# A fused decoder step: the transpose of the maxima moved behind its step's scores, three roots moved to GpSimd, first values and sample rows issued later

## The chip, the cores and the metric

The kernel runs on one core of one Trainium2 chip. The metric is the device time of one execution in microseconds (us). The engines are PE (TensorE, matrix products), ACT (ScalarE), DVE (VectorE), POOL (GpSimd) and SP (SyncE, which issues the DMAs). Each engine works through its own queue in order, so an instruction that waits holds everything behind it on its engine.

## The reference

One layer of a hybrid decoder for two groups of rows: a prompt of 1024 tokens (8 tiles of 128) and 8 sample sequences of 4 tokens (32 rows, the ninth tile). All is float32.

1. h = RMSNorm(x) @ w_in is split into gMLP inputs u and v, a query latent cq (256), a key-value latent ckv (256) and a rope key (32). Group A is a chunked gMLP. Group B is latent attention with 8 heads of 64 + 32 dimensions: q = RMSNorm(cq) @ w_uq, k = ckv @ w_uk joined with the rope key, v = ckv @ w_uv, with an RMSNorm of q and k per head, a rotation of the last 32 dimensions, and a softmax. Prompt rows attend causally to the prompt. The rows of each sample attend to 4096 cached positions (32 pages of 128 from a page table) and to themselves. Both groups' outputs are RMS-normalised, joined and multiplied with w_o.
2. Memory attention, 4 heads, 256 memory tokens.
3. A gated FFN with a causal convolution of width 3.

Outputs are both groups' rows, and the new latents, keys and states.

## The kernel before

Float32 products are made of three matmuls each (`mm3`, L179-185): both operands are split into a rounded high part and the low rest (`split`, L187-202: the high part on ACT, the low part on DVE), and high x high, high x low, low x high are summed in PSUM. Nearly all rows of PE in the profile therefore have line L185. Reciprocal roots are made from simple operations by `rsqrt_steps` (L214-245): with no engine given, 11 operations on DVE; with GpSimd given, 3 on DVE and 13 on GpSimd.

The stages, in order: phase 1 (norms, w_in, gMLP), phase 2a (prompt attention), phase 2b (sample attention over the cache), output projection, memory attention, FFN. The change touches phases 2a and 2b. In the other stages a scheduler sets the order when the kernel is built; in the two loops below the order on PE, ACT, DVE and POOL is the order of the code.

**Start of phase 2a (L596-655).** `proj_group` (L795-858) returns two lists for a group of tiles and four heads (hf 0 or 1): first queries and keys with their squares, norms and rotations, and second the values (6 matmuls of 128x256 for each tile, copied from PSUM by ACT, L815). For hf 0 all groups, (0,2), (2,4), (4,6), (6,8) and the sample rows (8,9), run both lists here, with PSUM tiles of the tag "mm" (5 buffers). Then the pools ps1 and p2x are closed, ps2 is opened, and `head_prep` (L860-876) transposes keys and queries of head 0 on PE (L872; two times four tiles each) and splits them. `proj_weights` for hf 1 follows, with its splits (w q and w v, low parts on DVE, L192).

**The attention loop of phase 2a.** 32 units (head, pair of query tiles) are worked through in 80 slots t. A slot of the loop issues transposes of the probabilities (L918, copied to pth by ACT, L920), the scores of the unit two ahead (L185, tile s; the maximum and the copy on DVE, L899 and L903; the exponential on ACT, L909), the products with the values (L930), and whatever stands in `extra[t]`, where `spread` puts head preparations and the projections of hf 1. POOL makes weight sums for the FFN (L770-773) in every fourth slot from 22 on. When 28, 29 and 30 units are done, a *mixer* (`mix_steps`, L1479-1505) starts for G = 0, 2 and 1: ACT squares two tiles with a sum per row (L1490), the root of the 128x2 sums (mixr) is made on DVE, ACT scales by it (L1496), PE transposes (L1501), DVE copies (L1502), and SP stores the result. These three are the only calls that give the arguments z = 1 and a function nt.

**Phase 2b (L1048-1169).** 8 batches of 16 steps, n from -10 on; step n scores two pages (`pair_score`: 12 matmuls of 128x288 into the two banks of tile s, then 12 of 128x256 into a third, tile s2; each tag has two buffers). `at(n, pos, f)` registers f for a position of a step, and a step runs: positions -2, -1, 0, the rotation of a coming quad's keys, position 1, the step's scores, position 2, in every fourth step 8 products with the cached latents (`quad_pv`, L1348), position 3. What pair_score leaves for the next step (the rope copy L1253, and the sums ss of L1278) runs at position -1 of it. The rope matmul L1250 of every second step writes into the new tile s.

The softmax of a batch is spread over steps by `batch_softmax` (L1282-1339) in eleven parts r, at the positions of L1082, counted from the batch's first step: r = 0 to 3 norms and scaling of pages 0 to 23, r = 4 their maxima, r = 5 and 6 the same for the rest (ends with the joined maxima mx, L1323), r = 7 the transpose of the maxima on PE (L1326), r = 8 on DVE their maximum over partitions (L1329) and a diagonal matrix dg (L1331), r = 9 on PE a matmul that broadcasts it (L1334), an ACT copy bc (L1336) and a subtraction on POOL (L1337), r = 10 the exponential on ACT. Parts that fall behind the last step go to a list `late` in their order; that is so from r = 7 on for the last batch.

Of the kernel before, what the change touches and what calls it, by code (L numbers as in the profile page):

```python
# [154 lines left out]
class Net:  # L155
# [440 lines left out]
    def phase2a(self):  # L596
        nc, tc, I, O = self.nc, self.tc, self.I, self.O
        p = self.open("p2q")
# [4 lines left out]
        p = self.open("p2")  # L603
        pp = self.pools["ps1"][1]
        px = self.open("p2x")
        heads = lambda: {"v": self.t(p, [P, 8, 4, 64], F32, "v", 2)}
        st = [{**heads(), **self.wqv}]
# [34 lines left out]
        rq = self.t(p, [P, 8, 8], F32, "rq")  # L642
        c = {"ggq": ggq, "cmask": cmask, "rq": rq, "kss": kss, "qt": qt}
        groups = ((0, 2), (2, 4), (4, 6), (6, 8), (8, 9))
        for g in groups:
            for f in sum(self.proj_group(p, pp, 0, *g, st[0], c, ("mm", 5)), []):
                f()
        self.close("p2x")
        self.close("ps1")
        pp = self.open("ps2", space=PSUM)  # L650
        pm = self.open("p2m")
        for f in self.head_prep(pm, pp, 0, st[0], c):
            f()
        st.append({**heads(), **self.proj_weights((pm, [P, 512], F32, "pth", 5), 1)})


# [2 lines left out]
        def spread(fs, t0, t1):  # L659
            for j, f in enumerate(fs):  # L660
                extra[t0 + j * (t1 - t0) // len(fs)].append(f)

        for h in (1, 2, 3, 5, 6, 7):
            fs = self.head_prep(pm, pp, h, st[h // 4], c)
            if h == 3:
                for f, t in zip(fs, (13, 14, 15, 19)):
                    extra[t].append(f)
            else:
                spread(fs, max(0, 10 * h - 16), 10 * h - 8 if h > 1 else 3)
        late = [self.proj_group(p, pp, 1, *g, st[1], c) for g in groups]  # L670
        for (q, _), t in zip(late, ((16, 20), (18, 23), (21, 26), (24, 29))):
            spread(q, *t)
# [7 lines left out]
        with tc.manual_schedule(engines={E.PE, E.Activation, E.DVE, E.Pool}):  # L680
# [30 lines left out]
            for n, u in enumerate(units):  # L711
                nu = units[n + 2] if n + 2 < len(units) else None
                k = u["n"]
# [334 lines left out]
    def phase2b(self):  # L1048
        nc, tc, I = self.nc, self.tc, self.I
        pa = self.pa3 = self.open("p3a", side="right")  # L1050
        pt, p = self.open("p3t"), self.open("p3")
        ppt, pp = self.open("ps3t", space=PSUM), self.open("ps3", space=PSUM)
# [11 lines left out]
        st, ev, late = {}, {}, []  # L1064

        def at(n, pos, f, *a):
            ev.setdefault((n, pos), []).append(lambda: f(*a))
# [10 lines left out]
        for b in range(NB):  # L1078
            n = b * 16
            at(n - 10, 0, lambda b: st.__setitem__(b, self.batch_open(p, b)), b)  # L1080
            at(n - 8, 2, lambda b: self.batch_enter(st[b], b), b)
            for r, (k, pos) in enumerate(((12, 0), (13, 0), (14, 0), (14, 3), (15, 0), (16, 0), (16, 2), (18, 0), (18, 3), (19, 2), (20, 2))):  # L1082
                f = lambda b=b, r=r: self.batch_softmax(p, ppt, st[b], r, b == NB - 1)
                if n + k <= last:
                    at(n + k, pos, f)
                else:
                    late.append(f)
            n += 16 + LAG + 15
            tail = (
                lambda b=b: self.batch_out(pt, st[b], 0),  # L1090
                lambda b=b: self.batch_out(pt, st[b], 1, ppt),
                lambda b=b: self.batch_close(pt, ppt, b, st.pop(b)),
            )
            for k, pos, f in ((0, 3, tail[0]), (1, 2, tail[1]), (3, 3, tail[2])):
                if b < NB - 1:
                    at(n + k, pos, f)
# [382 lines left out]
    def mix_steps(self, p, pp, z, i0, i1, src, hl, nt, tt):  # L1479

        nc = self.nc
        t0, tn, m = TILES[i0][0], TILES[i1 - 1][1], i1 - i0
        r = self.t(p, [P, 2], F32, "mixr", 2)[:tn, :m]
        ns = []
        for i in range(i0, i1):

            n = nt(i - i0)[:tn] if nt else src(i)[:tn]
            ns.append(n)
            o = n if nt else hl[:, 2 * (i - i0) : 2 * (i - i0) + 2].rearrange("p k n -> p (k n)")[:tn]
            nc.scalar.activation(o, src(i)[:tn], AF.Square, accum_out=r[:, i - i0 : i - i0 + 1])  # L1490
        yield
        self.rsqrt(p, r, r, 1.0 / 512)
        w = m * tn
        yield
        for i, n in enumerate(ns):
            nc.scalar.activation(n, src(i0 + i)[:tn], AF.Copy, scale=r[:, i : i + 1])  # L1496
        yield
        for i, n in enumerate(ns):
            tp = self.t(pp, [P, 512], F32, *tt).rearrange("p (k n) -> p k n", k=4)[:, :, :tn]
            for k in range(4):  # L1500
                nc.tensor.transpose(tp[:, k], n[:, k * P : k * P + P], self.ident[:tn, :tn])  # L1501
            nc.vector.tensor_copy(hl[:, :, i * tn : i * tn + tn], tp)  # L1502
            if nt is None and i < m - 1:
                yield
        nc.sync.dma_start(self.mix_dram[:, z * 4 : z * 4 + 4, t0 : t0 + w], hl[:, :, :w])
# [779 lines left out]
```

## Time and profile before

| | |
|---|---|
| median of 3 runs | 1880.57 us (1879.95 to 1886.6) |
| the profiled execution | 1887.48 us |
| its span, first to last instruction | 1885.8 us |
| mean granted TensorE clock | 0.985 |
| PE busy | 1822.9 us |
| DVE, ACT, POOL busy | 1380.2, 927.5, 715.1 us |
| phase 2a, first score of the loop | at 221.7 us |
| phase 2b, one batch of 16 steps | 57.40 us |

Times in the profile are us from the first instruction. A row of a timeline gives start, length, engine, line, operation, "output<-inputs" by the program's names, partitions x elements, a count, and in brackets how long the engine was idle before it and which instruction ended that. PEclk is the share of full speed that TensorE's clock was granted. PEld is PE's loading of weights, beside its matmuls. Lines are those of the kernel before.

### The profile page before, as it was taken

To read this page: it belongs to the slowest core of one execution; us is meant where nothing else is said; L and a number is where in the kernel's file an instruction comes from. 1 tells how busy PE (TensorE), PEld (TensorE's weight loads), DVE (VectorE), ACT (ScalarE), POOL (GpSimd) and SP (SyncE) were. 2 spreads that over 40 slices of the span, in tenths; PEclk is the share of its full clock that TensorE was granted. 3 is DMA by queue.
4 is the path that set the end of the run, shared out by engine and by line. 5 is a ranking of instruction groups with operands and counts; after the bars stand their busy time and mean duration, and the time that the engine had idled before them with its cause. 6 is when DMAs were issued, how large, how long until landed. Compare 5 with 4: busy or idle time off the path is not lost.

```text
span 1885.8 us, 39848 instructions
## 1 busy us (share of the span) xinstructions
PE 1822.9 (97%) x14402; PEld 1757.2 (93%) x14402; DVE 1380.2 (73%) x2883; ACT 927.5 (49%) x1965; POOL 715.1 (38%) x826
## 2 busy tenths in 40 slices
PE   6999899989999999999999999999999999999999
PEld 6999799889999999998799988999999999999999
DVE  6865967766777667776654676788888888879664
ACT  6435676666555555555443355633332333344442
POOL 1221515643544455444213100157677677500000
PEclk9999899999999999999999999999999999999999
DMA  8102204666765665664564335322222222395252
GB/s 294 60 10 69 80 1 163 228 223 186 213 196 167 187 179 169 175 170 148 171 177 134 134 134 163 128 80 69 91 69 94 77 69 80 99 363 164 79 153 76
DMA packets 135559, 260.18 MB, mean 138 GB/s; under 512 B 20417, under 2 KB 78626, under 8 KB 132290
## 3 DMA queue, kind: packets, MB, share of 16 engines
q1 hardware_dynamic: 134498, 256.58, 43.4%
q8 instruction: 114, 1.87, 0.4%
q10 hardware_dynamic: 864, 1.05, 0.2%
q14 instruction: 83, 0.68, 0.1%
HBM read 212.27 MB, written 45.30 MB: 137 GB/s over the span
## 4 chain that ended last, share of the span: by engine, by line
PE 60%; DVE 6%; issue 4%; DMA 3%; POOL 2%; SPq 1%; ACT 1%; POOLq 0%; DVEq 0%; ACTq 0%
PE d L185 12%; PE s L185 11%; PE b L185 7%; PE F L185 7%; PE X L185 6%; PE E L185 6%; PE A L185 3%; PE y L185 3%; DMA cT<-cT 1%; PE o L1348 1%; DVE mx L1299 1%; POOL S L1296 1%; PE t L185 1%; PE v L185 1%; SPq L1207 1%
## 5 line engine op out<-in xcount | busy, mean ns | idle before, releaser
L185 PE MATMUL s<-w2h,ch 128*128 128x288 f32 (+1 forms) x1024 | 303.8, 297 | 0.0
L185 PE MATMUL s<-w2h,cl 128*128 128x288 f32 (+1 forms) x1024 | 295.1, 288 | 2.7 <-POOL cl L1235 1.4
L185 PE MATMUL s<-w2l,ch 128*128 128x288 f32 (+1 forms) x1024 | 294.7, 288 | 0.0
L185 PEld LDWEIGHTS s<-w2h,ch 128*128 128x128 f32 x1024 | 192.6, 188 | 10.8 <-issue 8.3
L185 PEld LDWEIGHTS s<-w2h,cl 128*128 128x128 f32 x1024 | 192.4, 188 | 3.4 <-POOL cl L1235 1.9
L185 PEld LDWEIGHTS s<-w2l,ch 128*128 128x128 f32 x1024 | 192.8, 188 | 0.0
L1278 DVE TENSOR_REDUCE ss<-sq 128x16 f32<-128x1024 f32 x128 | 155.6, 1215 | 49.3 <-ACT sq L1275 48.4
L1235 POOL TENSOR_TENSOR cl<-cT,ch 128x512 fp32r<-128x512 f32 x64 | 83.7, 1307 | 160.7 <-ACT ch L1231 128.9
L1275 ACT ACTIVATE sq<-s 128x512 f32<-128x512 f32 x128 | 76.5, 598 | 90.0 <-PE s L185 90.0
L1272 ACT ACTIVATE sq<-s 128x512 f32<-128x512 f32 x128 | 76.8, 600 | 78.0 <-PE s L185 78.0
L191 ACT CAST a<-brb 128x528 fp32r<-128x528 f32 x77 | 48.8, 634 | 111.0 <-PE d L185 107.1
L185 PE MATMUL mm<-whi,xh 128*128 128x256 f32 (+3 forms) x288 | 84.5, 294 | 14.4 <-ACT xh L195 9.8
L185 PE MATMUL d<-a,w 128*128 128x264 f32 x768 | 95.4, 284 | 1.0 <-DVE G L2064 1.0
L192 DVE TENSOR_TENSOR a<-brb,a 128x528 fp32r<-128x528 f32 x77 | 54.4, 707 | 57.2 <-ACT a L191 57.1
L185 PEld LDWEIGHTS d<-a,w 128*128 128x128 f32 x768 | 94.3, 188 | 1.1 <-issue 1.1
L185 PE MATMUL mm<-wlo,xh 128*128 128x256 f32 (+3 forms) x288 | 83.3, 292 | 0.0
L185 PE MATMUL mm<-whi,xl 128*128 128x256 f32 (+3 forms) x288 | 83.2, 293 | 0.0
L930 PEld LDWEIGHTS o<-v,pth 128*128 128x128 f32 x576 | 75.9, 197 | 7.3 <-ACT pth L920 5.2
L930 PE MATMUL o<-v,pth 128*128 128x64 f32 x576 | 76.2, 274 | 4.8 <-ACT pth L920 4.4
L1935 POOL TENSOR_TENSOR lo<-s,hi 128x1024 fp32r<-128x1024 f32 x20 | 63.0, 3148 | 45.7 <-ACT hi L1934 45.7
L1231 ACT CAST ch<-cT 128x512 fp32r<-128x512 f32 x128 | 73.5, 627 | 3.9 <-DMA cT<-cT 3.9
L1990 ACT COPY a<-A 128x264 f32<-128x264 f32 x43 | 16.1, 375 | 118.7 <-PE A L185 114.9
(714 smaller groups left out, 6472.2 us busy)
## 6 DMA issues: line engine op xcount, KB each, us to landing
cT<-cT SPq DMA_DIRECT2D x256, 160.0 KB, 2.5
ck<-ck SPq DMA_DIRECT2D x256, 144.0 KB, 3.4
raw<-w_up SPq DMA_DIRECT2D x44, 512.0 KB, 3.6
wsumd<-wsum SPq DMA_DIRECT2D x13, 1024.0 KB, 4.3
actd<-cv SPq DMA_DIRECT2D x44, 264.0 KB, 2.6
brb<-actd SPq DMA_DIRECT2D x44, 264.0 KB, 5.9
wsum<-w_down SPq DMA_DIRECT2D x11, 1024.0 KB, 5.2
raw<-wsumd SPq DMA_DIRECT2D x20, 512.0 KB, 3.8
```

What stands on the lines that cost most here:

```text
L185: self.nc.tensor.matmul(out, l, r, start=first and i == 0, stop=last and i == len(seq) - 1)
L191: {"act": nc.scalar.copy, "pool": nc.gpsimd.tensor_copy, "dve": nc.vector.tensor_copy}[eng](hi, src)
L192: low = lambda: nc.vector.tensor_tensor(lo, src, hi, ALU.subtract)
L930: nc.tensor.matmul(u["o"][:, e], th[:, z * P : z * P + P], s["v"][:, jj, h % 4], start=j == z == 0, stop=e == 1 and jj == 2 * G + 1)
L1207: nc.sync.dma_start(ck[j * 32 : j * 32 + 32], I["ck"][bass.ds(rv, 1)].rearrange("a t s f -> (a t) s f"))
L1231: nc.scalar.copy(d["h"][:, k], src[k])
L1235: (nc.vector if k else nc.gpsimd).tensor_tensor(d["l"][:, k], src[k], d["h"][:, k], ALU.subtract)
L1272: nc.scalar.activation(sq[:, 0], ps[:, :, n0 : n0 + 256], AF.Square)
L1275: nc.scalar.activation(sq[:, 1], pt.rearrange("p (e d) -> p e d", e=2), AF.Square)
L1278: yield lambda: nc.vector.tensor_reduce(s["ss"][:, g0 : g0 + 2].rearrange("p e (z h) -> p z e h", z=2), sq.rearrange("p z e (h d) -> p z e ...
L1296: e.tensor_tensor(x, x, ss[:, g0:g1].rearrange("p g h -> p (g h)").unsqueeze(2).broadcast_to([P, n, 4]), ALU.mult)
L1935: eng.tensor_tensor(lo, src, hi, ALU.subtract)
```

## The change

Four edits. (1) For hf 0 only queries and keys of the groups (0,2) to (6,8) run before the pools change; their values run behind the preparation of head 0, in the PSUM tag "tp" (4 buffers). (2) The sample rows' queries and keys for hf 0 are spread over the slots 4 to 11 of the attention loop. (3) In the softmax of a batch, part 7 goes from step 18, position 0 to position 2; part 8 from step 18, position 3 to step 19, position 1; part 9 from step 19, position 2 to step 20, position 0; part 10 from step 20, position 2 to position 3. (4) The three late mixers of phase 2a make their roots with `rsqrt_steps` on GpSimd.

```diff
-        for g in groups:
-            for f in sum(self.proj_group(p, pp, 0, *g, st[0], c, ("mm", 5)), []):
+        for g in groups[:4]:
+            for f in self.proj_group(p, pp, 0, *g, st[0], c, ("mm", 5))[0]:
                 f()
         self.close("p2x")
         self.close("ps1")
...
         for f in self.head_prep(pm, pp, 0, st[0], c):
             f()
+        for g in groups[:4]:
+            for f in self.proj_group(p, pp, 0, *g, st[0], c)[1]:
+                f()
         st.append({**heads(), **self.proj_weights((pm, [P, 512], F32, "pth", 5), 1)})
...
+        spread(self.proj_group(p, pp, 0, 8, 9, st[0], c)[0], 4, 12)
         late = [self.proj_group(p, pp, 1, *g, st[1], c) for g in groups]
...
-            for r, (k, pos) in enumerate(((12, 0), (13, 0), (14, 0), (14, 3), (15, 0), (16, 0), (16, 2), (18, 0), (18, 3), (19, 2), (20, 2))):
+            for r, (k, pos) in enumerate(((12, 0), (13, 0), (14, 0), (14, 3), (15, 0), (16, 0), (16, 2), (18, 2), (19, 1), (20, 0), (20, 3))):
...
-        self.rsqrt(p, r, r, 1.0 / 512)
+        for _ in self.rsqrt_steps(p, r, r, 1.0 / 512, nc.gpsimd if z and nt else None):
+            pass
```

## The prediction

> **What bounds the kernel now.** I read the page's busy shares first, then the waits of PE, then the stretches in which those waits lie. The page:
>
> ```profile
> PE 1822.9 (97%) x14402; PEld 1757.2 (93%) x14402; DVE 1380.2 (73%) x2883; ACT 927.5 (49%) x1965; POOL 715.1 (38%) x826
> ```
>
> PE (the matrix engine) is busy 97% of the 1885.8 us span, so all that is left to win without removing matmuls is some 63 us of holes, and time at a reduced clock. None of the four edits removes a matmul. The waits of PE (us in total, times, longest):
>
> ```profile
> PE m L1326 <- DVE mx L1323: 6.3, 7, 0.9
> PE o L930 <- ACT pth L920: 4.4, 1, 4.4
> PE tp L872 <- DVE rqa L234: 2.3, 1, 2.3
> ```
>
> The first is the transpose of the maxima, once for each of 7 batches. The second lies where the three late mixers stand. The third lies at the start of the attention, behind the first values and the sample rows. So each edit touches a known hole, and I price each hole alone.
>
> **Edit 3, the maxima.** Steps 49 to 52 of batch 2, PE, then DVE, ACT and POOL (start, length, operation):
>
> ```profile
> 610.84 0.28 PE L185 MATMUL s<-w2h,cl 128*128 128x256 f32 x1
> 612.06 0.29 PE L1326 MATMUL m<-ident,mx 128*32 128x128 f32 x1 [0.94 <-DVE mx L1323]
> 615.18 0.38 PE L1250 MATMUL s<-bd,krq 128*128 128x128 f32 x2
> 618.49 0.40 PE L1334 MATMUL m<-dg,ones 32*128 32x32 f32 x2
> 618.83 1.07 PE L1348 MATMUL o<-ck,S 128*32 128x257 f32 x16
> 619.83 0.40 PE L185 MATMUL s<-w2h,ch 128*128 128x288 f32 x1
> ...
> 613.92 0.21 DVE L1274 TENSOR_TENSOR S<-s,S 128x64 f32<-128x64 f32 x1
> 616.45 0.33 DVE L1331 TENSOR_SCALAR dg<-ident,mm 32x32 f32<-32x32 f32 x1
> 617.01 0.71 DVE L1235 TENSOR_TENSOR cl<-cT,ch 128x512 fp32r<-128x512 f32 x1 [0.23 <-issue]
> 617.64 1.21 DVE L1278 TENSOR_REDUCE ss<-sq 128x16 f32<-128x1024 f32 x1
> 618.77 0.27 DVE L1244 TENSOR_REDUCE kss<-ksq 128x4 f32<-128x128 f32 x1
> ...
> 614.16 0.27 ACT L1253 COPY S<-s 128x128 f32<-128x128 f32 x1 [2.41 <-DVE S L1274]
> ```
>
> The transpose (position 0 of step 50) stands ahead of step 50's scores and waits 0.94 us for the maxima; 24 score matmuls are queued behind it. Moved to position 2 it stands behind them, and the maxima have 3 us to spare. But the 0.94 us does not all come back. Step 51 begins with L1250, which writes a scores buffer; there are two, and the one it takes is free when ACT's rope copy L1253 has read step 49's (614.16 + 0.27 = 614.43). That copy waits for DVE's addition at 613.92, which the edit does not make earlier. Without the hole L1250 would come at 615.18 - 0.94 = 614.24, so it now waits until about 614.5: gain so far 0.68.
>
> The diagonal dg (r = 8) goes from position 3 of step 50 to position 1 of step 51, behind cl, ss and kss: 617.01 to 619.04 in the rows above. As its own 0.6 us now follow them, dg ends at about 619.06 less the part of the 0.68 that DVE's operations follow: 618.6 to 619.06, I take 618.95. The broadcast L1334 (r = 9) goes behind the value matmuls of L1348, which end about 618.83 + 1.0 - 0.34 (the broadcast that no longer precedes them) - 0.68 = 618.8. So the broadcast starts at about 618.95, takes 0.34, and step 52 starts at about 619.25 instead of 619.83: gain 0.6. Over 7 batches (the last batch's steps are in the late list, unmoved): **-4.2 us**. The ends are -6.6 (the whole wait, 7 x 0.94) and 0 (the rope copy and dg eat it all). A loss I exclude here: the exponentials are first read some three steps later, 9 us at the 3.1 us from L1326 to L1250, while copy, subtraction and exponential come to this:
>
> ```profile
> 619.35 2.48 POOL L1337 TENSOR_TENSOR S<-S,bc 128x1056 f32<-128x1056 f32 x1 [1.27 <-ACT bc L1336]
> ```
>
> and an exponential of the same tile on ACT, at most as much again. Behind the waiting transpose stands nothing but the rest of PE's queue, and it no longer waits.
>
> **Edit 4, the roots on GpSimd.** At the end of the attention loop, ACT, DVE (the first row groups the three roots' first operations: min/median/max ns, first and last start), POOL and PE:
>
> ```profile
> 418.15 1.32 ACT L1496 ACTIVATE k<-b_all,mixr 128x512 f32<-128x512 f32 x2
> 420.60 1.04 ACT L920 COPY pth<-tp 128x512 f32<-128x512 f32 x2
> 425.90 1.33 ACT L1496 ACTIVATE k<-b_all,mixr 128x512 f32<-128x512 f32 x2
> 429.66 1.34 ACT L1496 ACTIVATE k<-b_all,mixr 128x512 f32<-128x512 f32 x2
> ...
> L222 DVE TENSOR_SCALAR rqx<-mixr x3: 158/169/170, 411.5 to 425.6; 128x2 f32<-128x2 f32 x3
> 414.48 0.16 DVE L236 SCALAR_TENSOR_TENSOR mixr<-rqh,rqy 128x2 f32<-128x2 f32 x1
> ...
> 417.20 1.27 POOL L773 TENSOR_TENSOR wsum<-wsum 128x512 f32<-128x512 f32 x1
> 418.49 0.45 POOL L1220 TENSOR_TENSOR krq<-cT,cosT 128x128 f32<-128x128 f32 x1
> ...
> 421.21 1.08 PE L930 MATMUL o<-v,pth 128*128 128x64 f32 x4 [4.43 <-ACT pth L920]
> ```
>
> The first late mixer's root is ready at 414.64 on DVE; ACT reads it at 418.15 (L1496), then squares for the next mixer, then copies pth, for which PE sits idle 4.43 us. From ACT's L1496 to PE's end of idling are 3.06 us in a fixed order. Each root keeps 3 of its 11 DVE operations and gets 13 on GpSimd: 3 x 8 = 24 DVE operations go, 39 GpSimd ones come. In the order of the changed kernel all 39 stand behind the last weight sum, which ends at 417.20 + 1.27 = 418.47. So the root that was 3.5 us early is now late by whatever its 13 operations take, and L1496 holds ACT, pth and PE behind it.
>
> No GpSimd operation on 128x2 stands in this trace. The nearest rows, a copy of 128x16 (min/median/max ns) and two steps of a root on 128x64:
>
> ```profile
> L2044 POOL COPY S<-state x22: 193/198/573, 1210.1 to 1608.0; 128x16 f32<-128x16 f32 x22
> ...
> 909.99 0.32 POOL L243 TENSOR_TENSOR rqh<-rqh,rqa 128x64 f32<-128x64 f32 x1
> 910.40 0.37 POOL L244 TENSOR_SCALAR rqh<-rqh 128x64 f32<-128x64 f32 x1
> ```
>
> 0.45 for 128 elements and 0.32 for 64 make about 0.2 at 2 elements, as the copy has it; the two steps start 0.41 apart, 0.09 beyond the first one's length, so I take 0.28 apart. The first root is then ready at 418.47 + 13 x 0.28 = 422.1, L1496 is 3.95 late, and PE with it. The second root starts when its squares are done, about 420.7 as pth follows them at 420.60, and has 425.90 - 420.7 = 5.2 us for 3 DVE operations (0.6) and 13 on GpSimd (3.6), so it is in time; the third has 429.66 - 425.6 = 4.0 and is 0.2 late. **+4.1 us.** Ends: 0.16 apart, a DVE operation's length, gives +2.4; 0.41 apart, as at 128x64, gives 418.47 + 5.3 = 423.8, +5.65, and the third root is then 1.9 late, +7.6 in all. That DVE is freed earlier brings nothing, as ACT waits for the root, not for DVE. The Trainium skill (GPSIMD Engine Reference, section 3.1) has a tensor_tensor on GpSimd 1.96 times as long as on VectorE, in a measurement with large tiles; by that and DVE's rows here, about 0.32 to 0.4 apart, this term would be an estimated +4.5 to +5.7 instead; no run here shows it at two elements.
>
> **Edits 1 and 2, the start of the attention.** Stretches, in busy us of PE, PEld, DVE, ACT, POOL, then PEclk (granted clock), DMA share and GB/s:
>
> ```profile
> 216.50:221.40 4.90, 2.34 (x10) 1.87 (x10) 4.87 (x26) 1.99 (x5) 1.13 (x1) 0.50 0.02 9
> 221.40:226.00 4.60, 4.33 (x14) 3.50 (x15) 4.57 (x21) 1.88 (x6) 0.00 (x0) 0.50 0.00 0
> 226.00:233.50 7.50, 7.50 (x30) 6.87 (x29) 5.00 (x18) 3.22 (x7) 1.46 (x4) 0.50 0.01 2
> 417.00:421.20 4.20, 0.00 (x0) 0.00 (x0) 0.70 (x4) 4.20 (x10) 2.73 (x6) 1.00 0.47 199
> 421.20:428.10 6.90, 6.88 (x34) 6.89 (x34) 4.65 (x23) 3.63 (x9) 0.00 (x0) 0.51 0.31 109
> ```
>
> DVE is full up to 226 and PE waits for it; the clock is half from 216.5 to 233.5. Before, the values (48 matmuls) lie inside this DVE-bound stretch and cost nothing; after, they stand among the first scores, where PE is full:
>
> ```profile
> 211.23 0.28 PE L185 MATMUL mm<-wvh,ckh 128*128 128x256 f32 x1
> 211.94 0.33 PE L185 MATMUL mm<-wqh,cqh 128*32 128x384 f32 x1
> 221.72 0.46 PE L185 MATMUL s<-kTh,qTh 96*128 96x128 f32 x1
> 234.42 0.37 PE L185 MATMUL s<-kTh,qTl 96*128 96x448 f32 x1
> ```
>
> The first row is the first of the last value's six matmuls, the second follows them: 0.71 us, 0.118 each, so 48 make 5.7 us at full clock. The sample rows' 12 matmuls (211.94 to 213.84) move 1.9 us of PE into the loop as well; there they displace nothing but PE's own queue. In return the first score needs neither the last keys' transposes, nor the sample rows' chain, nor the weight splits ahead of it on DVE; counting those (some 4 to 6 us of the chain that ends at 221.40), I put it at 216.0 instead of 221.72. From the first score to the row at 234.42 PE had 12.7 us of work, 11.8 of it at half clock: 5.9 + 0.9 = 6.8 at full clock. With 5.7 + 1.9 it is 14.4. If the half clock lasts 6.9 us as at 421.20, until 222.9, 3.45 of the 14.4 are done by then and the rest takes 10.95, to 233.85 instead of 234.42: **-0.6 us**. The ends: the 12.1 us that it lasted after 221.40 give 216.0 + 12.1 + 8.35 = 236.45, +2.0; a clock that never drops gives 230.4, -4.0. The Trainium skill (TensorE: Matmul & The Clock Gate, Part 1) says that the first 3.4 us or so of activity run at half clock and everything after at full; the stretches above show 6.9 and 12.1. By that rule the term would be an estimated -2.3, between this forecast and the third rival.
>
> **The rest.** The output projection and the memory attention hold the same instructions in a slightly other order that the scheduler chose; I see no sign for either, 0 with ±3.
>
> Sum: -4.2 + 4.1 - 0.6 = **-0.7 us**. The profiled execution took 1887.5 (1885.8 of span, 1.7 around it) and would take 1886.8; the median of the three runs is 1880.57, lower by 7, and since the edits' terms are short waits and not shares, I take them off it unscaled: **1879.9 us**.
>
> **Rivals.**
> - *The GpSimd roots cost more* (ends on the slower side). One mechanism: each small operation on GpSimd takes as long as at 128x64. Then edit 4 is +7.6 and the sum +2.8: 1883.4. It decides from about 0.30 us apart: 0.32 + 13 x 0.30 = 4.2 and the third root's 0.5 make 4.7, against the 4.8 that the other edits give. For it: the rows at 128x64; against: the copy's 0.2. Beside busy DVE work the same root's steps took much longer (min/median/max ns):
>
> ```profile
> L239 POOL TENSOR_TENSOR rqa<-rqa,rqx x2: 1185/1246/1307, 899.3 to 906.1; 128x64 f32<-128x64 f32 x2
> ```
>
> So long, the first root alone would make 13 x 1.25 = 16 and a sum of +12: 1892; but DVE does nearly nothing in 417.00:421.20.
> - *The maxima's wait only changes its name.* Rope copy, dg and the DVE backlog behind them end at the same time as before; edit 3 gives 0, the sum is +3.5: 1884.1. For it: dg is now behind 2 us of DVE work. Against: DVE stood idle ahead of cl.
> - *The clock stays up at the attention's start*, since PE pauses less: -4.0 instead of -0.6, sum -4.1: 1876.5; with the cheap ends of the other two, -6.6 + 2.4 - 4.0 = -8.2, 1872.4.
>
> **How the numbers follow.** Forecast 0.45, dear roots 0.25 (of which 0.05 for 1892), renamed wait 0.15, clock 0.15 (of which 0.05 near 1872). Predicted is the likeliest, 1879.9. The range from 1872 to 1888 holds all but about 0.2: the ends of the terms together, -11 and +13 (with the 3 of the rest), less their least likely corners. A measurement here tells about 0.5%, 9.4 us, from no change. Faster by more than that needs all gains at once: 0.07; slower by more needs the dear roots under traffic, or a transfer pushed back in a queue: 0.10; within: 0.83.
>
> **What the changed kernel's profile would show.** Right: the wait at L1326 gone, small ones at L1250 (for ACT's rope copy) and at the broadcast (for dg), step 52 about 0.6 earlier after step 49; PE's wait for pth about 8 us instead of 4.43, with ACT's scaling waiting for a POOL result; first score near 216, half clock to about 223. Wrong: the wait for pth under 7 us or over 10; a batch as long as before, 57.40 us for 16 steps in this row:
>
> ```profile
> 599.00:656.40 57.40, 56.46 (x479) 53.12 (x478) 42.25 (x81) 32.11 (x72) 27.59 (x43) 1.00 0.64 177
> ```
>
> It would also be wrong if the output projection moved by more than 3 us.

## The result and the profile after

The changed kernel takes 1888.3 us (median of 13 runs; two of them, at 5.2 and 6.2 ms, were disturbed and stand outside the comparison, and the other 11, 1886.07 to 1891.78, have the median 1888.1). The kernel before takes 1884.0 us (13 runs, 1879.95 to 1886.71). The ratio of the two, without those two runs, is 1.0027, 95% interval 1.0017 to 1.0037: **slower by 5.1 us** (0.0027 x 1884), 3.2 to 7.0. Forecast was -0.7 us.

The page of the changed kernel's profile (span 1885.5 us) and its waits of PE (us in total, times, longest). Its lines are numbered four or five higher than before: the transpose is L1330, cl L1239, the wait for pth L934, the rope matmul L1254.

```profile
PE 1819.1 (96%) x14402; PEld 1755.0 (93%) x14402; DVE 1377.8 (73%) x2859; ACT 927.2 (49%) x1965; POOL 722.6 (38%) x865
```

```profile
PE s L185 <- DVE cl L1239: 7.1, 7, 1.3
PE o L934 <- ACT pth L924: 7.0, 1, 7.0
...
PE tp L876 <- DVE k L852: 3.4, 1, 3.4
PE s L1254 <- DVE rsum L939: 2.6, 1, 2.6
```

The 7 waits for the maxima (6.3 us) are gone; 7 waits for cl (7.1 us) stand in their place. The wait for pth grew from 4.4 to 7.0. At the first rope matmul of the sample attention PE now waits 2.6 us, where before it waited 1.26 for a cl a little further on:

```profile
437.24 0.40 PE L185 MATMUL s<-w2h,cl 128*128 128x288 f32 x1 [1.26 <-DVE cl L1235]
```

So each of the holes has a successor as large or larger.

**Batch 2, steps 50 to 52 of the changed kernel**, DVE, then PE and ACT:

```profile
614.45 0.19 DVE L1327 TENSOR_TENSOR mx<-mx 128x32 f32<-128x32 f32 x1
614.62 0.69 DVE L1239 TENSOR_TENSOR cl<-cT,ch 128x512 fp32r<-128x512 f32 x1
616.55 0.21 DVE L1278 TENSOR_TENSOR S<-s,S 128x64 f32<-128x64 f32 x1
621.08 0.23 DVE L1335 TENSOR_SCALAR dg<-ident,mm 32x32 f32<-32x32 f32 x1
```

```profile
615.37 0.40 PE L185 MATMUL s<-w2h,cl 128*128 128x288 f32 x1 [0.98 <-DVE cl L1239]
617.81 0.27 PE L1330 MATMUL m<-ident,mx 128*32 128x128 f32 x1
617.92 0.39 PE L1254 MATMUL s<-bd,krq 128*128 128x128 f32 x2
621.24 1.07 PE L1352 MATMUL o<-ck,S 128*32 128x257 f32 x16
622.24 0.41 PE L1338 MATMUL m<-dg,ones 32*128 32x32 f32 x2
```

The low half cl of a quad is made in two parts, the first on POOL and the second on DVE (`quad_prep`). The sixth matmul of step 50, the row at 615.37, is the first to read the second part, and DVE makes that part directly behind the last operation on the maxima. Before, the transpose waited for the maxima and cl was ready a moment later; now five scores go ahead of the transpose, and the sixth waits 0.98 us for cl, where the transpose waited 0.94.

What this does to a batch is read from broadcast to broadcast, with one trap. In the kernel before the broadcast stands ahead of the value matmuls of its step, in the changed kernel behind them (621.24, then 622.24 above). The first batch has no values of an earlier batch there, so between its first two broadcasts the kernel before has three sets of 16 value matmuls and the changed one four (55.63 and 57.09 us). Between later broadcasts both have four: the mean of these five times is **57.53 us instead of 57.44**. The mean over all six, 57.46 instead of 57.14, counts the extra set as a loss.

**The late mixers of the changed kernel**, POOL, ACT, DVE and PE:

```profile
411.30 1.27 POOL L777 TENSOR_TENSOR wsum<-wsum 128x512 f32<-128x512 f32 x1
412.52 0.20 POOL L238 TENSOR_TENSOR rqa<-rqy 128x2 f32<-128x2 f32 x1
415.99 0.19 POOL L245 TENSOR_TENSOR mixr<-rqh,rqy 128x2 f32<-128x2 f32 x1
```

```profile
416.22 1.33 ACT L1501 ACTIVATE k<-b_all,mixr 128x512 f32<-128x512 f32 x2 [2.74 <-POOL mixr L245]
...
428.24 1.33 ACT L1501 ACTIVATE k<-b_all,mixr 128x512 f32<-128x512 f32 x2 [0.68 <-POOL mixr L245]
```

```profile
433.87 1.29 DVE L1507 COPY v<-tp 128x512 f32<-128x512 f32 x2 [4.32 <-DMA mix<-v]
```

```profile
419.30 1.97 PE L934 MATMUL o<-v,pth 128*128 128x64 f32 x8 [7.01 <-ACT pth L924]
435.30 0.46 PE L1254 MATMUL s<-bd,krq 128*128 128x128 f32 x2 [2.61 <-DVE rsum L939]
```

The first root begins on POOL when the last weight sum ends, takes 3.66 us (412.52 to 416.18), and ACT waits for it. The third is 0.68 late. Behind them the last mixer's copy out of PSUM waits for the DMA that stores an earlier one, and the first rope matmul waits until that copy and what follows it on DVE (rsum, at 435.07) are done.

**The attention's start in the changed kernel** (columns as before; PEclk is the third from the end):

```profile
204.00:207.00 3.00, 3.00 (x14) 3.00 (x13) 3.00 (x14) 1.15 (x3) 2.46 (x7) 0.50 0.82 226
211.00:214.00 3.00, 1.90 (x8) 1.45 (x8) 2.86 (x10) 0.38 (x1) 2.44 (x4) 0.50 0.89 359
214.00:221.00 7.00, 6.65 (x32) 6.63 (x32) 4.57 (x18) 2.49 (x7) 0.62 (x1) 0.52 0.00 1
221.00:226.00 5.00, 5.00 (x42) 4.85 (x41) 2.20 (x7) 3.57 (x13) 0.00 (x0) 1.00 0.00 0
```

```profile
214.36 0.47 PE L185 MATMUL s<-kTh,qTh 96*128 96x128 f32 x1 [0.35 <-ACT qTh L195]
230.95 0.37 PE L185 MATMUL s<-kTh,qTl 96*128 96x448 f32 x1
```

The first score comes 7.4 us earlier (214.36 for 221.72), the scores of 448 columns 3.5 us earlier (230.95 for 234.42).

### The profile page after: what moved, and what is told of

It is laid out like the page before. It is cut to its first block, busy times and chain, and to the rows that moved or that the text cites. A ratio compares the mean times of both kernels' runs of the same rounds, so it can differ in the third digit from the quotient of the medians.

```text
span 1885.5 us, 39860 instructions
## 1 busy us (share of the span) xinstructions
PE 1819.1 (96%) x14402; PEld 1755.0 (93%) x14402; DVE 1377.8 (73%) x2859; ACT 927.2 (49%) x1965; POOL 722.6 (38%) x865
## 4 chain that ended last, share of the span: by engine, by line
PE 63%; DVE 5%; issue 4%; DMA 2%; POOL 2%; SPq 1%; ACT 1%; DVEq 0%; POOLq 0%; ACTq 0%
PE s L185 12%; PE d L185 12%; PE b L185 8%; PE X L185 7%; PE F L185 7%; PE E L185 7%; PE A L185 3%; PE y L185 3%; PE o L1352 1%; DVE mx L1303 1%; POOL S L1300 1%; DMA cT<-cT 1%; PE t L185 1%; PE v L185 1%; PE s L1254 0%
## 5 line engine op out<-in xcount | busy, mean ns | idle before, releaser
L1239 POOL TENSOR_TENSOR cl<-cT,ch 128x512 fp32r<-128x512 f32 x64 | 83.2, 1300 | 150.8 <-ACT ch L1235 135.8
L934 PEld LDWEIGHTS o<-v,pth 128*128 128x128 f32 x576 | 75.0, 196 | 9.6 <-ACT pth L924 7.8
L934 PE MATMUL o<-v,pth 128*128 128x64 f32 x576 | 75.6, 273 | 7.1 <-ACT pth L924 7.0
```

What stands on the lines that cost most here:

```text
L934: nc.tensor.matmul(u["o"][:, e], th[:, z * P : z * P + P], s["v"][:, jj, h % 4], start=j == z == 0, stop=e == 1 and jj == 2 * G + 1)
L1239: (nc.vector if k else nc.gpsimd).tensor_tensor(d["l"][:, k], src[k], d["h"][:, k], ALU.subtract)
```

## The experiments

**Which edit costs.** Each edit was put alone into the kernel before.

e1, edit 3 alone:

```diff
-(18, 0), (18, 3), (19, 2), (20, 2)
+(18, 2), (19, 1), (20, 0), (20, 3)
```

> The kernel before with edit 3 alone (the maxima's transpose and what follows it later). Theory A: the low half cl of the next quad stands right behind the maxima on DVE, so step 50's third matmul waits for it as long as the transpose waited before: no wait at L1326, 7 waits of about 1 us for cl (7.1 us in the changed kernel), each batch 0.0 to 0.2 us longer; in all 0 to +1 us. Theory B, as predicted: the maxima's wait was the limit, edit 3 gives -4.2 us, and what the changed kernel lost it lost to the roots and at the start of the sample attention: -3 to -5 us.

Measured: ratio 1.0005 (0.9992 to 1.0018), +0.9 us (-1.5 to +3.4); waits for cl 7.9 us (8, one of them at the start of the sample attention), none at the transpose; a batch 57.50 us (mean of five, as above), 0.06 longer. Theory A, but that it is the sixth matmul that waits; the forecast's -4.2 is excluded.

e2, edit 4 alone:

```diff
-        self.rsqrt(p, r, r, 1.0 / 512)
+        for _ in self.rsqrt_steps(p, r, r, 1.0 / 512, nc.gpsimd if z and nt else None):
+            pass
```

> The kernel before with edit 4 alone (three roots on GpSimd). Theory A: 13 operations 0.28 us apart behind the last weight sum; PE's wait for pth 7.0 to 8.4 us instead of 4.4, the third root some 0.7 late: +2.5 to +4.5 us. Theory B: the late roots only fill time that PE would lose anyway at the start of the sample attention (where the first quads' loads and the last mixer's store end): 0 to +1 us.

Measured: 1.0017 (1.0006 to 1.0028), +3.2 us. Theory A, with a longer wait than expected; the wait for cl at the start of the sample attention also grew, from 1.26 to 2.23 us, as the last mixer's copy comes later. POOL, ACT and PE:

```profile
413.83 1.26 POOL L773 TENSOR_TENSOR wsum<-wsum 128x512 f32<-128x512 f32 x1
415.05 0.19 POOL L238 TENSOR_TENSOR rqa<-rqy 128x2 f32<-128x2 f32 x1
...
418.74 1.33 ACT L1497 ACTIVATE k<-b_all,mixr 128x512 f32<-128x512 f32 x2 [6.72 <-POOL mixr L245]
...
421.81 1.97 PE L930 MATMUL o<-v,pth 128*128 128x64 f32 x8 [9.36 <-ACT pth L920]
```

e3, edits 1 and 2; e8, edit 1 alone; e9, edit 2 alone:

```diff
-        for g in groups:
-            for f in sum(self.proj_group(p, pp, 0, *g, st[0], c, ("mm", 5)), []):
+        for g in groups[:4]:                                  # e3, and e8 with the sample rows behind it
+            for f in self.proj_group(p, pp, 0, *g, st[0], c, ("mm", 5))[0]:
...
+        for g in groups[:4]:                                  # in place of `for g in groups`, both lists: e9
...
+        for g in groups[:4]:                                  # behind head_prep: e3, e8
+            for f in self.proj_group(p, pp, 0, *g, st[0], c)[1]:
...
+        spread(self.proj_group(p, pp, 0, 8, 9, st[0], c)[0], 4, 12)   # e3, e9
```

> The kernel before with edits 1 and 2 (values and sample rows later). Theory A: 3.4 us won at the scores of 448 columns, of which the sample rows' 12 matmuls take back 1.8; the ten more PSUM tiles of the tag tp turn its four buffers by two, so that the first rope matmul of the sample attention now waits about 2.6 us for the last mixer's copy out of its bank (in the changed kernel that wait is 2.6): +0.5 to +1.5 us in all. Theory B: that wait comes from the late roots and is absent here: -1.5 to -2 us.

> The kernel before with edit 1 alone (first values behind the first transposes; sample rows where they were). Theory A (values move from a stretch where PE waits for DVE into one where PE is full; the first scores come earlier by as much): between -1 and +1 us. Theory B (the values' place is what loses: PE has nothing to do while DVE works, so its clock halves earlier): +1 to +3 us, with half clock from about 203 on.

> The kernel before with edit 2 alone (sample rows into the loop's slots 4 to 11). Theory A: DVE's chain to the first score loses the sample rows' operations, some 2 us, and PE gets 1.8 us more in the loop: -1 to +0.5 us. Theory B (PE's 1.8 us is all that counts): +1.5 to +2 us.

Measured: both 1.0010 (0.9998 to 1.0021), values alone 1.0021 (1.0010 to 1.0031), sample rows alone 1.0034 (1.0021 to 1.0046). Each half alone costs more (+4.0 and +6.4 us) than both together (+1.9); the expectations for the halves failed but for theory B of the values: half clock comes at 204.5, and its +1 to +3 us overlaps the interval (1.9 to 5.8). The wait at the first rope matmul is there in e3 with the roots on DVE, as theory A has it, but 1.47 us long. Where it stands fits the number of new tiles of the tag tp, which has four buffers: e8 adds eight, two whole turns, and has no such wait (1.25 for cl, as before); e9 adds two and e3 ten, half a turn more, and have it, as do all seven profiles with edit 2 and none of the twelve without. The rows of e3 and e9:

```profile
435.83 0.46 PE L1254 MATMUL s<-bd,krq 128*128 128x128 f32 x2 [1.47 <-DVE rsum L939]
```

```profile
433.90 0.46 PE L1251 MATMUL s<-bd,krq 128*128 128x128 f32 x2 [0.88 <-DVE v L1503]
```

That turn costs some 0.2 us against the 1.25, so it is not what the halves cost; why they do not add is not settled.

**The maxima.** e5 puts part 6 (up to the joined maxima) behind cl as well; e11 moves the transpose alone, e12 part 6 alone; e10 adds to e5 one addition on POOL instead of DVE:

```diff
 positions of r = 6, 7, 8, 9, 10
-(16, 2), (18, 0), (18, 3), (19, 2), (20, 2)      # before
+(17, -1), (18, 2), (19, 1), (20, 0), (20, 3)     # e5, e10
+(16, 2), (18, 2), (18, 3), (19, 2), (20, 2)      # e11
+(17, -1), (18, 0), (18, 3), (19, 2), (20, 2)     # e12
...
-            e.tensor_tensor(x, x, s["kss"][:, g0:g1]...
+            (nc.gpsimd if g0 else e).tensor_tensor(x, x, s["kss"][:, g0:g1]...     # e10
```

> The kernel before with edit 3, and in addition part 6 of the softmax (the rest of the norms up to the joined maxima) one step later, step 17 position -1, so that cl stands ahead of the maxima on DVE; the transpose at step 18 position 2 still comes behind them. Theory A: the waits for cl go with those for the maxima; each batch is 0.6 to 0.95 us shorter, -4 to -6.5 us in all. Rival: the rope copy behind DVE's backlog and dg hold PE instead, 0 to -2 us, with waits named S (ACT) or dg (DVE).

> The kernel before with only the transpose of the maxima moved (part 7 to step 18, position 2; parts 8 to 10 where they were). Read from the time between two batches' broadcasts (57.13 us before, 57.35 with all of edit 3 alone). Theory A (PE waits for cl as long as it waited for the maxima, and the excess comes from dg and the broadcast behind step 51): 57.1 to 57.2. Theory B (the transpose itself in the new place costs): 57.3 to 57.4.

> The kernel before with only part 6 of the softmax moved behind cl, the transpose at its old place ahead of step 50's scores. Theory A (two results of one DVE queue are needed at the start of step 50, and whichever is last holds PE): the transpose now waits longer, 1.2 to 1.8 us instead of 0.94, and a batch takes 57.3 to 58.0 us. Theory B (cl alone was the limit): 56.7 as with both moved.

> The kernel of the run before with the maxima behind cl, and in addition the first addition of the second norms (1.1 us on DVE in its profile) on POOL, which is idle there. Theory A (what is left of the wait, 2.3 us at L1250 for ACT's rope copy, comes from DVE's backlog): that wait falls to under 0.5 us and the time is 1.5 to 2.5 us under that run's, -5 to -6 us against the kernel before. Theory B (the backlog follows PE and refills): the same -3 us as without it.

Measured, by the last five times between broadcasts: before 57.44 us a batch, e11 57.50, e1 57.50, e12 57.92, **e5 56.82**, e10 57.15. (The expectations count from the mean of all six; for e11 and e12 that changes nothing, as their broadcast stands in the old place.) So the transpose alone gains nothing, nor does all of edit 3; part 6 alone loses 0.5; both together gain 0.62 a batch, 4.3 us over 7. e5's ratio is 0.9983 (0.9970 to 0.9996), -3.2 us (-5.7 to -0.8): theory A by the batch, with the waits that the rival named in the place of those for cl. One wait was held by two results of one queue. DVE, ACT and PE of e5:

```profile
607.40 0.68 DVE L1235 TENSOR_TENSOR cl<-cT,ch 128x512 fp32r<-128x512 f32 x1
610.20 0.19 DVE L1323 TENSOR_TENSOR mx<-mx 128x32 f32<-128x32 f32 x1
611.63 0.21 DVE L1274 TENSOR_TENSOR S<-s,S 128x64 f32<-128x64 f32 x1
...
611.88 0.27 ACT L1253 COPY S<-s 128x128 f32<-128x128 f32 x1 [2.15 <-DVE S L1274]
...
611.93 0.27 PE L1326 MATMUL m<-ident,mx 128*32 128x128 f32 x1
612.29 0.46 PE L1250 MATMUL s<-bd,krq 128*128 128x128 f32 x2
```

cl is 3 us ahead now, and what is left is what the forecast had named: the rope copy and dg. Waits of PE in e5, 490 to 900 us, then, from the whole span, e12's at the transpose and e11's for cl:

```profile
PE s L1250 <- ACT S L1253: 2.3, 6, 0.9
PE m L1334 <- DVE dg L1331: 0.7, 1, 0.7
```

```profile
PE m L1326 <- DVE mx L1323: 10.5, 7, 2.0
```

```profile
PE s L185 <- DVE cl L1235: 8.0, 8, 1.5
```

e10 failed: the wait for the rope copy rose to 3.9 us (7) where it should have gone, and the ratio is 1.0004 (0.9994 to 1.0015). DVE waits for the addition on POOL (7 times, 2.9 us between 490 and 900), and the first step of the root behind it then runs beside POOL's half of cl and takes 1.26 or 1.27 us in each of the seven batches, where it took 0.35 in six of them in e5 (0.20 in the first, with POOL idle). DVE of e10, then of e5:

```profile
607.79 1.26 DVE L222 TENSOR_SCALAR rqx<-ss 128x64 f32<-128x64 f32 x1 [0.41 <-POOL ss L1289]
```

```profile
605.16 0.35 DVE L222 TENSOR_SCALAR rqx<-ss 128x64 f32<-128x64 f32 x1
```

**The roots' place in the queue.** e7 has edit 4 and every weight sum four slots earlier; e14 the earlier sums alone:

```diff
-            wsums = dict(zip(range(22, 75, 4), (NK, NK + 1, *range(NK))))
+            wsums = dict(zip(range(18, 71, 4), (NK, NK + 1, *range(NK))))
```

> The kernel before with edit 4, and every weight sum four slots earlier, so that the last one is over before the first root comes to POOL. Theory A (the roots are late because they stand behind the last weight sum; 13 operations at 0.28 us cost 1.5 us more than DVE's 11, which the slack holds): PE's wait for pth falls from 9.4 us with edit 4 alone to some 4 to 6, and the time comes within 1 us of the kernel before. Theory B (the operations themselves are too slow on POOL, wherever they stand): PE's wait stays over 8 us and the time stays 3 us above.

> The kernel before with the weight sums four slots earlier and nothing else. Theory A (the gain of the run with all edits and both repairs lies in the sums' place: a weight sum on POOL no longer falls where the loop's end needs POOL, DVE or the port they share): -2 to -4 us. Theory B (earlier sums alone change nothing; they only let the roots on GpSimd pay): -1 to +1 us.

Measured: e7 1.0008 (0.9994 to 1.0021), e14 1.0006 (0.9995 to 1.0017). The interval of e7 overlaps that of e2 (1.0006 to 1.0028), so the repair shows in the waits and not in the time. In e7 the sum is over 2 us before the first root, and PE's wait for pth is 2.6 us and 1.0 us instead of 9.4. POOL and PE of e7:

```profile
406.27 1.29 POOL L773 TENSOR_TENSOR wsum<-wsum 128x512 f32<-128x512 f32 x1
409.78 0.19 POOL L238 TENSOR_TENSOR rqa<-rqy 128x2 f32<-128x2 f32 x1 [2.22 <-DVE rsum L935]
...
416.55 1.10 PE L930 MATMUL o<-v,pth 128*128 128x64 f32 x8 [2.63 <-ACT pth L920]
```

The operations are the same, so what made the wait was the queue, not the engine. Sums alone gain nothing that shows (theory B).

**Mended versions.** e6: edits 1, 2 and 3 with part 6 behind cl. e13: all four edits, part 6 behind cl, earlier sums. e15: e13 without edit 4. e16: e13 without edits 1 and 2. Their lines are those above, in these combinations:

```diff
+ r = 6 at (17, -1)                 # e6, e13, e15, e16
+ wsums from range(18, 71, 4)       # e13, e15, e16
- roots on GpSimd                   # left out: e6, e15
- values and sample rows later      # left out: e16
```

> The changed kernel without the roots on GpSimd (edits 1, 2 and 3) and with part 6 of the softmax behind cl. If the parts add, by the medians of the runs alone: +1.9 (edits 1 and 2) - 3.2 (maxima behind cl) = -1.3 us, -4 to +1. If edits 1 and 2 cost nothing by themselves and their +1.9 was chance: -3.2.

> All four edits with both repairs: part 6 of the softmax behind cl, and the weight sums four slots earlier, so that the roots on GpSimd do not stand behind the last one. If the parts add: +1.9 - 3.2 + 1.5 (roots with earlier sums) = +0.2 us, -3 to +3, against +5.1 for the four edits as they are. PE's wait for pth under 5 us; batch 56.7 us.

> Edits 1, 2 and 3 with maxima behind cl and sums four slots earlier, roots on DVE: the best run without edit 4. Theory A (roots on GpSimd gain nothing by themselves): -5 to -7 us, as with them. Theory B (once they do not stand behind a weight sum the roots on GpSimd gain, as DVE's scores and value scalings no longer stand behind a root): -1 to -3 us, 4 us above the run with them.

> Edits 3 and 4 with both repairs, and the start of the attention as before (without edits 1 and 2). If edits 1 and 2 cost the +1.9 us of their run alone, this one is 2 us under the run with all four, -8 to -10 us. If they cost nothing or gain beside the others: -5 to -7 us.

Measured: e6 0.9995 (0.9980 to 1.0011), e13 **0.9962 (0.9949 to 0.9976), -7.1 us**, e15 1.0020 (1.0010 to 1.0030), e16 0.9999 (0.9986 to 1.0012). e6 is as the sum of the parts has it. e13 beats the kernel before and the sum (+0.2) by 7 us and the changed kernel, by the two ratios, by 12 (e13 ran on one chip, e15 and e16 on another, each beside the kernel before); taking out either the roots on GpSimd or the new start loses all of that. For e15 theory B holds in direction; for e16 neither does. All four kernels have a batch of 56.8 us (56.76 to 56.87, mean of five), so the batches do not tell them apart. What does is not found: the profile of e13 is of an execution that took 1884.4 us, 5.6 above the median of its runs, and can't show where its gain lies.

**The same kernels profiled once more.**

```diff
 (no change: e17 is the kernel before, e18 the changed one)
```

> The kernel before, profiled once more, to see what of a stage's time belongs to the code and what to the clock. Theory A (the half clock comes in whole steps of some 3.4 us whose start is free, so stages with a hole in PE vary from run to run by 1.7 us a step, and the others do not): against the first profile the attention's start, the stretch around 310, the mixers and the output projection differ by up to 3 us each, batches (57.14) and the FFN by under 0.1. Theory B (the stages' times belong to the code): all within 0.3 us.

> The changed kernel, profiled once more. Theory A: its mixers' stage is again some 4 us longer than that of kernels with roots on DVE and its batches again 57.4 to 57.5 us, while the attention's start and the output projection move by up to 3 us against its first profile. Theory B: all stages within 0.3 us of its first profile.

The table gives how much longer a stage of PE took than in the first profile of the kernel before, measured between the same two matmuls (named by their times there).

| kernel | 160 to 281: start | 281 to 360 | 409 to 480: mixers | 480 to 880: batches | 880 to 1000: out |
|---|---|---|---|---|---|
| before again (e17) | -2.5 | -1.3 | -1.6 | +0.1 | -0.5 |
| changed | -0.8 | -2.9 | +6.1 | +1.0 | -3.2 |
| changed again (e18) | -0.8 | -1.3 | +4.3 | +1.7 | -1.7 |
| e1, edit 3 | -2.6 | -1.3 | +3.0 | +1.2 | -2.5 |
| e2, edit 4 | -2.5 | -1.3 | +4.6 | +0.4 | -2.1 |
| e3, edits 1 and 2 | -2.1 | +0.2 | +1.3 | +0.3 | +0.7 |
| e5 | -2.4 | -1.3 | +0.7 | -2.3 | -2.0 |
| e6 | -2.0 | +0.2 | +4.7 | -3.5 | -1.3 |
| e9, edit 2 | +0.4 | +0.2 | -1.8 | +1.0 | +1.6 |
| e13 | +1.4 | +0.9 | -2.6 | -3.3 | +1.8 |
| e15 | +1.2 | +0.8 | -1.1 | -2.2 | -0.6 |
| e16 | -0.4 | +2.3 | -1.8 | -4.0 | +1.3 |

Theory A holds for both in these stages. One kernel's stages with a hole in PE differ by up to 2.5 us between two executions; its batches agree (57.44 and 57.41, mean of five; changed 57.53 and 57.55). The stretches of e17 that answer to the first row of the changed start above and to those shown in the prediction:

```profile
204.00:207.00 3.00, 2.09 (x13) 2.04 (x14) 2.90 (x9) 3.00 (x20) 3.00 (x8) 1.00 0.82 224
221.40:226.00 4.60, 4.60 (x16) 3.79 (x16) 4.06 (x21) 2.08 (x6) 0.00 (x0) 0.50 0.00 0
226.00:233.50 7.50, 7.50 (x47) 6.77 (x46) 5.98 (x19) 5.91 (x13) 1.46 (x4) 0.92 0.01 2
```

In the first profile the last of these was at 0.50 throughout. Differences of up to some 2.5 us in a stage with a hole are therefore no evidence from one profile. The mixers' stage shows edit 4 only on the mean: 5.0 in the three profiles with the roots behind the weight sum (6.1, 4.3, 4.6), 1.2 in the eleven with the roots on DVE and the sums in their old places (-1.8 in e9 to +4.7 in e6), so 3.8, near the forecast 4.1.

## Why the prediction was wrong

The sign and the size of the sum failed, at one step above all, and the time lies just above the range. From the median of 13 runs the same sum gives 1883.3, and the range moves up with it: the baseline decided on which side of the bound the time fell, but not the sign.

- **Edit 3 (-4.2 forecast, the step that failed).** The prediction has "24 score matmuls are queued behind it" and "the maxima have 3 us to spare", and never asks what those matmuls themselves need. The sixth of them needs the part of cl that DVE makes right behind the maxima, and waits 0.98 us for it. So PE is not released 0.94 us earlier, from which the step reckoned on. Measured: +0.1 us a batch in the changed kernel, +0.06 in e1, and +0.9 us (-1.5 to +3.4) for edit 3 alone, so the term was about 5 us too low. A batch as long as before was the sign of being wrong that the prediction itself had named. The rival that the wait would only change its name came true (0.15 was given), by cl and not by the rope copy or dg. What the step said of those two was right: with cl out of the way e5 waits for just them and gains 0.62 a batch, against the forecast 0.6.
- **Edit 4 (+4.1).** Right in mechanism and size: 13 operations in 3.66 us (forecast 3.64), behind the last weight sum, PE's wait 7.0 (forecast about 8), third root 0.68 late (0.2). Alone it measured +3.2 (1.1 to 5.3), and with the sum out of the way the wait shrank to 2.6. GpSimd at two elements costs 0.19 to 0.23 us and 0.28 apart, as the row of 128x16 gave; the dearer rival had the wrong neighbour, and the 1.96 that the Trainium skill (GPSIMD Engine Reference, section 3.1) gives for large tiles does not carry down to two elements: a tensor_tensor took 0.19 to 0.20 us on GpSimd and 0.16 on DVE, 1.2 times.
- **Edits 1 and 2 (-0.6).** The first score came even earlier than forecast (214.36 for 216.0) and the half clock ended at about 221 (222.9). But the gain was reckoned against an execution whose half clock lasted 17 us; in e17 it ended some 6 us sooner (0.92 in the last row above is 1.2 us of half clock), and the start of the kernel before took 2.5 us less. Against that one the changed start loses 1.7 us (-0.8 against -2.5). The term also put the half clock at 6.9 us from the first score on. In the changed kernel it lasted 10.2 us, from 210.5 to 220.7, and 3.4 us more from 203.7, ahead of the first score, where the prediction has none: with the values gone PE was busy 2.06 us from 200 to 204, against 3.45 in e17. All seven profiles with edit 1 have half clock between 200 and 208, none of the twelve without it has. What it costs is not worked out. The two edits measured +1.9 (-0.4 to +4.0): wrong by 2.5, in the baseline of the term and in the length of the half clock.
- **Not in the sum.** The wait at the first rope matmul, 2.61 us (2.25 in e18) against 1.26 before. Two causes add: the turned tp buffers (e3, 1.47) and the last mixer's later copy with roots on GpSimd (e2, 2.23 for cl, and no less with earlier sums: 2.37 in e7). The part on edit 4 followed the root to ACT and PE and did not follow it to the copy behind it.
- **The rest** (0 ±3): -3.2 and -1.7 in the output projection, but e2, in which PE's order there is that of before, shows -2.1 too, so nothing of it is put down to the new order. The sign of being wrong that the prediction named, more than 3 us, stood in the first profile and not in the second.
- **The baseline.** 1880.57 was the median of three runs; over 13 it was 1884.0. That moved the forecast time, not the difference.

The terms as measured alone, +0.9 (edit 3) + 3.2 (edit 4) + 1.9 (edits 1 and 2), make 6.0 against 5.1 (3.2 to 7.0); the intervals of the first and the last hold 0 as well. What stays open is why e13 gains 7 us: not the sums alone (e14), and not without the roots on GpSimd (e15) or without the new start (e16).

## What to carry to other kernels

When an instruction that waits is moved behind others, look at what those others wait for, and on which queue it is made: here the next operand came off the same DVE queue one operation later, and only moving producer and consumer together (the maxima behind cl, their transpose behind the scores) won 0.62 us a batch and 3.2 us in all (e5). When a batch is measured between two marks, see that the same work stands between them in both kernels: here a mark that moved past the value matmuls made 0.1 us look like 0.32. An engine that is idle on the average is not free at the place: the same 13 small operations cost PE 7 to 9 us of waiting behind a weight sum and 2.6 without one, where the roots on DVE cost 4.4. And a single profile of a kernel with holes in PE is one draw: compare the stages that repeat (here the batches, good to 0.03 us between two executions), and take a second profile before pricing a hole.

## What the runs showed of the hardware

The half clock came in steps. Adding up the 1 us windows below full clock at the attention's start gave 17.1 us (before), 10.2 (before again, e1, e2, e5), 13.7 (changed, both times) and 6.8 (e7); around 310 it was 0, 3.4 or 6.8 us in kernels with the same 2.1 us hole. All are multiples of 3.4 us, each worth 1.7 us of PE's work where PE is full. The Trainium skill (TensorE: Matmul & The Clock Gate, Part 1) has a free-running window of about that length, which agrees. Its rule that everything after the first 3.4 us or so runs at full clock fits the 3.4 us cases, not those where PE was busy and half clocked for two windows (6.88 of 6.90 us at 421.20).

DVE beside GpSimd: the same operation on 128x64 took 1.26 to 1.27 us on DVE while GpSimd ran a tensor_tensor on 128x512 (e10, seven times), 0.35 beside its smaller ones on 128x128 (e5, six times) and 0.18 to 0.20 with GpSimd idle (both kernels).
